# Latent attention on one core: second keys, values, head fillers and output pieces in another order

## The chip, the cores and the metric

The kernel runs on 1 core of one Trainium2 chip. The metric is device time in microseconds (us) of one execution. The kernel before took 850.55 us in the median of 3 runs (849.61 to 850.91).

## What is computed

Two transformer blocks over 256 tokens of width 1024: sliding-window attention and a gated feed-forward network, then an mLSTM and spatial-gating mixer, a feed-forward network, **latent attention**, and a last feed-forward network. Only the latent attention's order changes. Its computation, with 16 heads, 64 plain and 32 rotary features per head:

```python
def mla_mixer(h, positions, w_in, q_g, kv_g, w_uq, w_ukv, w_out):
    cq, ckv, kr = jnp.split(h @ w_in, [Q_LORA, Q_LORA + KV_LORA], axis=-1)
    q = (rms_norm_2(cq, q_g) @ w_uq).reshape(bsz, seq, C_HEADS, C_NOPE + C_ROPE)
    kv = (rms_norm_2(ckv, kv_g) @ w_ukv).reshape(bsz, seq, C_HEADS, C_NOPE + C_V)
    ...
    q_rope = apply_rope(q[..., C_NOPE:], cos, sin)
    k_rope = apply_rope(kr[:, :, None, :], cos, sin)
    qf = jnp.concatenate([q[..., :C_NOPE], q_rope], axis=-1)
    kf = jnp.concatenate([kv[..., :C_NOPE], jnp.broadcast_to(k_rope, ...)], axis=-1)
    v = kv[..., C_NOPE:]
    ...
        s = jnp.einsum("bqhd,bkhd->bhqk", qblk, kf) * scale
        pr = jax.nn.softmax(s, axis=-1)
        o = jnp.einsum("bhqk,bkhd->bqhd", pr, v)
    return o @ w_out
```

## The kernel before

All weights stream once through the core. The host packs them into units of at most 128 x 1024 numbers in the order of their use (`_weights`); SyncE loads two units at a time (`raw`, 1 MB, three buffers), and each unit is split by ScalarE into a rounded high part `wh` (line 262) and by VectorE into the rest `wl` (line 263); nine such pairs fit. A product of activations and weights is three matmuls: high by high, low by high, high by low (`mm3`, line 295; every matmul of that kind has line 293). Activations are split in the same way (`split`, lines 311 to 315: `kb` for the key latents, `xb` for the query latents, `hb` for the heads' outputs). Transposes on TensorE have line 303. PSUM has eight tiles, all called `ps`.

A scheduler sets the order of each engine's instructions from the order in the code, priorities, and what it thinks to be ready; each engine then takes its list strictly from the top and waits where an operand is missing. `self.pin` keeps the weight splits where the code has them; `self.limit` and `self.ahead` say how many units may be split ahead.

Latent attention (`mla`, line 1111) has these steps. `mla_latent` (1125) makes key latents, query latents and the shared rotary key, normalizes them and transposes the key latents (`lck`, 1160). The rotary key goes to all heads of `kT` by a DMA (1195). `mla_keys` (1213) makes the plain keys of eight heads: 24 matmuls, whose results ScalarE (1220) and VectorE (1221) copy into `kT`. `cq_finish` (1197) transposes the query latents (`lcq`). `mla_heads` (1224) then runs the heads: `rope(g4)` makes the rotary queries of four heads (ScalarE copies them to `qr`, line 1253, VectorE shuffles, 1255, GpSimd multiplies by the cosines, 1256, VectorE adds into `qT`, 1259, four adds, one for each head), `nope(g4)` their plain part (copied by ScalarE, 1240), `values(n)` half of the values (24 passes of 512 columns in all for n = 0 and 1), `soft(h)` the scores and the softmax of a head (maximum 1286, exponentials 1291, division 1295), `trans(h)` transposes the probabilities (copied at 1305), and `value(j)` multiplies two heads by the values. `out_steps` (408) gives the eight pieces of the output projection, by output half n and input quarter kp; `boundary` (377) adds them to x, transposes x and hands over to the feed-forward network.

In the code before, the keys of heads 8 to 15 come first in `mla_heads`, then rotary and plain queries of the first four heads, `values(0)`, and the loop over the heads.

Of the kernel before, what the change touches and what calls it, by code (L numbers as in the profile page):

```python
# [18 lines left out]
P = 128  # L19
# [18 lines left out]
def _pb(w, cols):  # L38
    k = w.shape[0] // P
    return w[:, cols].reshape(k, P, len(cols)).transpose(1, 0, 2).reshape(P, -1)  # L40


def _pa(w, k0, k1, c0, c1):
    return w[k0 * P : k1 * P, c0:c1].reshape(k1 - k0, P, c1 - c0).transpose(1, 0, 2).reshape(P, -1)


def _rng(a, b):
    return np.arange(a, b)


def _pair_heads(j):
    p, g = divmod(j, 4)
    return 2 * p * 4 + g, (2 * p + 1) * 4 + g


def _out_units(w):
    return [_pa(w, 2 * kp, 2 * kp + 2, 512 * n, 512 * n + 512) for n in range(2) for kp in range(4)]


def _ffn_order(nf, nin):  # L60
# [10 lines left out]
def _weights(i):  # L71
    u = []
    w = i["swa_w_in"][0]
    for p in range(2):
        u.append(_pb(w, _rng(1024 + p * P, 1024 + p * P + P)))
    for h in range(2):
        u.append(_pa(w, 4 * h, 4 * h + 4, 1280, 1536))
    for j in range(8):
        a, b = _pair_heads(j)
        u.append(_pb(w, np.concatenate([_rng(a * 64, a * 64 + 64), _rng(b * 64, b * 64 + 64)])))  # L80
    w = i["swa_w_out"][0]
    rows = np.concatenate([_rng(h * 64, h * 64 + 64) for j in range(8) for h in _pair_heads(j)])
    u += _out_units(w[rows])
    wg, wd = i["ffn_w_gate_up"][0], i["ffn_w_down"][0]
    for kind, f, s in _ffn_order(FF1 // P, 2):
        if kind == "i":
            u.append(_pb(wg, _rng(s * FF1 + f * P, s * FF1 + f * P + P)))
        else:
            u.append(wd[f * P : f * P + P])
    w = i["ab_w_in_2"][0]  # L90
    g = np.zeros((D, P), w.dtype)
    for q, r in ((1, 0), (3, 32), (0, 64), (2, 96)):
        g[:, r : r + 4] = w[:, 2048 + 4 * q : 2048 + 4 * q + 4]
    u.append(_pb(g, _rng(0, P)))
    for h in range(4):
        for s in range(2):
            c = s * 512 + h * P
            u.append(_pb(w, _rng(c, c + P)))
    for c in (1024, 1536, 2576):
        for kp in range(4):  # L100
            u.append(_pa(w, 2 * kp, 2 * kp + 2, c, c + 512))
    for m in range(4):
        u.append(_pb(w, _rng(2064 + m * P, 2064 + m * P + P)))
    u += _out_units(i["ab_w_out_2"][0])
    for layer in range(2):
        w1, w2 = i["ffn_w1_2"][layer], i["ffn_w2_2"][layer]
        if layer == 1:
            w = i["c_w_in_2"][0]
            for k0 in (0, 4):
                for c0, c1 in ((384, 672), (0, 384)):  # L110
                    u.append(_pa(w, k0, k0 + 2, c0, c1))
                    u.append(_pa(w, k0 + 2, k0 + 4, c0, c1))
            w = i["c_w_ukv_2"][0]
            for m in range(0, 8, 4):
                u.append(np.concatenate([_pb(w, np.concatenate([_rng(h * P, h * P + 64) for h in (2 * a, 2 * a + 1)])) for a in range(m, m + 4)], 1))
            vc = np.concatenate([_rng(h * P + 64, h * P + P) for h in range(NH)])
            wv = [w[kt * P : kt * P + P][:, vc] for kt in range(2)]
            w = i["c_w_uq_2"][0]
            for g4 in range(4):
                ms = [np.concatenate([_rng(h * 96, h * 96 + 64) for h in (2 * a, 2 * a + 1)]) for a in (2 * g4, 2 * g4 + 1)]  # L120
                ms.append(np.concatenate([_rng(h * 96 + 64, h * 96 + 96) for h in range(4 * g4, 4 * g4 + 4)]))
                u.append(_pb(w, ms[2]))
                u.append(np.concatenate([_pb(w, ms[0]), _pb(w, ms[1])], 1))
                if g4 == 0:
                    u += wv
            u += _out_units(i["c_w_out_2"][0])
        for kind, f, s in _ffn_order(FF2 // P, 1):
            if kind == "i":
                u.append(_pb(w1, _rng(f * P, f * P + P)))
            else:  # L130
                u.append(w2[f * P : f * P + P])
    sizes = [a.shape[1] for a in u]
    if len(u) % 2:
        u.append(np.zeros((P, UN), np.float32))
        sizes.append(0)
    out = np.zeros((len(u) // 2, P, 2, UN), np.float32)
    for n, a in enumerate(u):
        out[n // 2, :, n % 2, : a.shape[1]] = a
    return out.reshape(len(u) // 2, P, 2 * UN), sizes
# [71 lines left out]
class K:  # L211
# [1011 lines left out]

    def mla_heads(self, ckT, cqT, kT, qsc):
        nc = self.nc
        self.mla_keys(ckT, kT, 1)
        qTs, prs, pts = {}, {}, {}
        acts = []
        v = [self.t([P, D], "mlv", 2) for _ in range(2)]
# [13 lines left out]
        def rope(g4):  # L1243
            qT = qTs[g4] = self.t([96, 4, T], "qT", 2)
            w = self.unit()
            ps = self.ps()
            for k in range(3):
                s = slice(k * P, k * P + P)
                self.mm3(ps[:, :T], (w[0][:, s], w[1][:, s]), cqT[k], k == 0, k == 2)
            self.done(w)  # L1250
            with self.tc.high_priority(100) if g4 == 0 else nullcontext():
                q0 = self.t([P, T], "qr0", 2)
                nc.scalar.activation(q0, ps[:, :T], AF.Copy)
                q1 = self.t([P, T], "qr1", 2)
                nc.vector.stream_shuffle(q1, q0, self.swap)
                nc.gpsimd.tensor_tensor(out=q0, in0=q0, in1=self.cosT, op=ALU.mult)
                nc.vector.tensor_tensor(out=q1, in0=q1, in1=self.sinT, op=ALU.mult)
                for e in range(4):
                    nc.vector.tensor_tensor(out=qT[64:96, e], in0=q0[32 * e : 32 * e + 32], in1=q1[32 * e : 32 * e + 32], op=ALU.add)  # L1259
# [3 lines left out]
        def values(n):  # L1263
            if n == 0:
                wv.extend((self.unit(), self.unit()))
            for t in range(2):
                ps = self.ps()
                for k in range(2):
                    s = slice(t * P, t * P + P)
                    c = slice(n * 512, n * 512 + 512)  # L1270
                    self.mm3(ps, (ckT[k][0][:, s], ckT[k][1][:, s]), (wv[k][0][:, c], wv[k][1][:, c]), k == 0, k == 1)
                nc.scalar.activation(v[t][:, n * 512 : n * 512 + 512], ps, AF.Copy)
            if n == 1:
                for w in wv:
                    self.done(w)
# [22 lines left out]
        def trans(h):  # L1298
            pr = prs.pop(h)
            tp = self.ps()  # L1300
            for kb in range(2):
                for t in range(2):
                    self.tr(tp[:, (kb * 2 + t) * P : (kb * 2 + t + 1) * P], pr[:, t, kb * P : kb * P + P])
            pt = self.t([P, 2, T], "mpt", 3)
            nc.scalar.activation(pt.rearrange("p a b -> p (a b)"), tp, AF.Copy)
            pts[h] = pt

        def value(j):
            p = [pts.pop(2 * j), pts.pop(2 * j + 1)]
            o = self.ps()  # L1310
            for kb in range(2):
                for e in range(2):
                    h = 2 * j + e
                    self.mm(o[e * 64 : e * 64 + 64, :T], v[kb][:, h * 64 : h * 64 + 64], p[e][:, kb], kb == 0, kb == 1)
            acts.append(self.split(o[:, :T], None, "h", 8))

        steps, accs = self.out_steps(acts, {1: lambda: trans(14), 2: lambda: (trans(15), value(6)), 3: lambda: value(7)})
        self.pin = True
        first = self.used
        self.limit = first + 7  # L1320
        self.ahead = WBUFS
        rope(0)
        nope(0)
        values(0)
        for h in range(NH):
            self.limit = first + 7 + min(h, 3) + (h >= 9) + (h >= 13)
            self.load()
            soft(h)
            if h >= 3:
                trans(h - 3)  # L1330
            if h == 0:
                values(1)
            if h in (0, 4, 8):
                rope(h // 4 + 1)
            if h in (1, 5, 9):
                nope(h // 4 + 1)
            if h >= 5 and h % 2 == 1:
                value((h - 5) // 2)
            if h == 10:
                steps[0].pop(0)()  # L1340
        trans(13)
        self.limit = 1 << 30
        self.pin = False
        self.ahead = 4
        return steps, accs


    def finish(self, acc, pend, down, tiles, r2):
# [86 lines left out]
```

## Time and profile before

| what | value |
|---|---|
| median of 3 runs | 850.55 us (849.61 to 850.91) |
| the profiled execution | 851.47 us, of it 849.8 us from the first instruction to the last |
| TensorE (PE) busy | 835.0 us, 98% of the span |
| VectorE (DVE) busy | 606.6 us, 71% |
| ScalarE (ACT) busy | 510.5 us, 60% |
| GpSimd (POOL) busy | 41.5 us, 5% |
| latent attention in the trace | from about 564 us to about 662 us |

How to read it: times in the trace count from the span's first instruction. PE's busy time is modelled with a matmul's latency in it, so that a row of matmuls overlaps; a wait shorter than that latency doesn't show as idle time. In brackets behind an instruction stands how long its engine had been idle before it and what ended that. A matmul of plain 32-bit numbers (scores, values times probabilities) runs as two passes, so two matmuls are four records.

### The profile page before, as it was taken

What the parts mean: (1) busy time and instruction counts of PE and PEld (TensorE: products, weight loads), DVE (VectorE), ACT (ScalarE), POOL (GpSimd) and SP (SyncE); (2) the same over time, 40 slices, a digit from 0 to 9 for tenths busy, and PEclk for the clock granted to TensorE, in tenths of its full rate; (3) what the DMA queues carried; (4) which work ended last, traced back from release to release, by engine and by line L of the source; (5) the groups of instructions that cost most, each with busy time, mean ns of one, the idle gap of its engine ahead of it and who ended that gap; (6) DMA issues with size and microseconds to landing.
All of it is one profiled execution on the core that took longest, in us unless ns stands there. A gap on an engine that the chain in (4) does not pass through costs nothing.

```text
span 849.8 us, 12664 instructions
## 1 busy us (share of the span) xinstructions
PE 835.0 (98%) x4768; PEld 721.3 (85%) x4768; DVE 606.6 (71%) x1135; ACT 510.5 (60%) x972; POOL 41.5 (5%) x58
## 2 busy tenths in 40 slices
PE   9999999999999999999999999999999999999996
PEld 9877888888888987988888888898877888888885
DVE  5897776666766897787666766667878766666644
ACT  6696655555455969866455645456787744545532
POOL 0520000000000002200000000001000000000001
PEclk9999999999999999999999999999999999999999
DMA  9447555555554514554655555545217655555511
GB/s 328 173 163 263 179 208 191 196 180 179 196 199 148 199 51 149 199 205 148 220 184 195 195 198 197 195 169 173 85 51 245 219 206 199 198 184 175 190 47 49
DMA packets 24109, 151.41 MB, mean 178 GB/s; under 512 B 2768, under 2 KB 3536, under 8 KB 6768
## 3 DMA queue, kind: packets, MB, share of 16 engines
q1 hardware_dynamic: 23712, 149.95, 49.8%
q8 instruction: 37, 0.61, 0.3%
q10 hardware_dynamic: 288, 0.52, 0.2%
q0 software_dynamic: 48, 0.13, 0.1%
q14 instruction: 24, 0.20, 0.1%
HBM read 149.03 MB, written 1.05 MB: 177 GB/s over the span
## 4 chain that ended last, share of the span: by engine, by line
PE 78%; DVE 10%; ACT 6%; DMA 3%; issue 2%; POOL 1%; SPq 0%; POOLq 0%; DVEq 0%; ACTq 0%
PE ps L293 76%; DVE wl L263 3%; DMA raw<-in_w_dram 3%; PE ps L303 2%; ACT wh L262 1%; DMA x<-in_x_dram 1%; DVE qk L888 1%; DVE xb L315 1%; DVE sws L723 1%; ACT mpr L1291 1%; DVE sws L704 1%; ACT L890 0%; DVE qT L1259 0%; POOL r L319 0%; ACT mex L994 0%
## 5 line engine op out<-in xcount | busy, mean ns | idle before, releaser
L263 DVE TENSOR_TENSOR wl<-raw,wh 128x1024 fp32r<-128x1024 f32 (+4 forms) x278 | 329.3, 1190 | 134.8 <-ACT wh L262 128.9
L262 ACT ACTIVATE wh<-raw 128x1024 fp32r<-128x1024 f32 (+4 forms) x278 | 284.2, 1032 | 136.3 <-PE ps L293 123.0
L293 PE MATMUL ps<-xb,wh 128*128 128x512 f32 (+1 forms) x1304 | 283.5, 356 | 1.2 <-ACT wh L262 0.7
L293 PE MATMUL ps<-wh,hb 128*128 128x512 f32 (+1 forms) x944 | 280.3, 379 | 0.3 <-ACT hb L311 0.3
L293 PEld LDWEIGHTS ps<-xb,wh 128*128 128x128 f32 x1304 | 215.6, 189 | 32.9 <-DVE xb L315 1.6
L293 PEld LDWEIGHTS ps<-wh,hb 128*128 128x128 f32 x944 | 169.1, 189 | 31.9 <-issue 1.7
L293 PE MATMUL ps<-wl,hb 128*128 128x512 f32 (+1 forms) x472 | 177.6, 377 | 0.5 <-DVE wl L263 0.5
L293 PE MATMUL ps<-xb,wl 128*128 128x256 f32 x1084 | 159.3, 282 | 0.0
L293 PEld LDWEIGHTS ps<-xb,wl 128*128 128x128 f32 x1084 | 150.5, 191 | 9.4
L311 ACT ACTIVATE hb<-fp 128x256 fp32r<-128x256 f32 x90 | 36.9, 415 | 119.2 <-DVE fp L545 89.7
L293 PEld LDWEIGHTS ps<-wl,hb 128*128 128x128 f32 x472 | 88.8, 188 | 17.3 <-DVE wl L263 0.9
L312 DVE TENSOR_TENSOR hb<-fp,hb 128x256 fp32r<-128x256 f32 x90 | 37.7, 424 | 33.9 <-ACT hb L311 33.9
L447 DVE TENSOR_TENSOR fg<-ps,fg 128x256 f32<-128x256 f32 x108 | 44.6, 417 | 10.4 <-ACT fg L446 10.4
L446 ACT ACTIVATE fg<-ps 128x256 f32<-128x256 f32 x108 | 39.9, 369 | 11.1 <-PE ps L293 11.0
L293 PE MATMUL ps<-wh,xb 128*128 128x512 f32 (+3 forms) x192 | 39.8, 350 | 0.0
L293 PEld LDWEIGHTS ps<-wh,xb 128*128 128x128 f32 x192 | 31.6, 189 | 3.5
L319 POOL TENSOR_TENSOR r<-ms,mhalf 128x2 f32<-128x2 f32 x7 | 5.3, 760 | 485.4 <-DVE ms L324 485.4
L545 DVE SCALAR_TENSOR_TENSOR fp<-fg 128x256 f32<-128x256 f32 x64 | 26.8, 423 | 1.8
L314 ACT ACTIVATE xb<-ps,cols 128x256 fp32r<-128x256 f32 x35 | 15.5, 470 | 18.8 <-PE ps L303 12.9
L315 DVE SCALAR_TENSOR_TENSOR xb<-ps,cols,xb 128x256 fp32r<-128x256 f32 x35 | 16.0, 479 | 9.6 <-ACT xb L314 9.5
L293 PE MATMUL ps<-wl,xb 128*128 128x512 f32 (+3 forms) x96 | 21.4, 348 | 0.0
L1291 ACT ACTIVATE mpr<-ps,mnm,qsc 128x256 f32<-128x256 f32 x32 | 17.8, 574 | 4.3 <-DVE mnm L1287 4.2
(224 smaller groups left out, 611.0 us busy)
## 6 DMA issues: line engine op xcount, KB each, us to landing
raw<-in_w_dram SPq DMA_DIRECT2D x135, 1024.0 KB, 4.7
raw<-in_w_dram SPq DMA_DIRECT2D x4, 512.0 KB, 7.2
xraw<-in_xt_dram SPq DMA_DIRECT2D x4, 257.0 KB, 4.9
raw<-in_w_dram SPq DMA_DIRECT2D x4, 256.0 KB, 5.6
x<-in_x_dram SPq DMA_DIRECT2D x4, 256.0 KB, 6.5
row_fn<-in_fn_dram SPq DMA_DIRECT2D x2, 512.0 KB, 6.2
kT<-kr SPq DMA_DIRECT2D x1, 512.0 KB, 4.6
out_dram<-fo SPq DMA_DIRECT2D x2, 256.0 KB, 2.0
```

Of the source, the lines that this page charges most:

```text
L262: a = self.nc.scalar.activation(hi[:, c], raw[:, c], AF.Copy)
L263: b = self.nc.vector.tensor_tensor(out=lo[:, c], in0=raw[:, c], in1=hi[:, c].bitcast(F32), op=ALU.subtract)
L293: self.nc.tensor.matmul(out, lhsT, rhs, start=start, stop=stop)
L303: self.nc.tensor.transpose(out, in_, self.ident)
L311: self.last_act = nc.scalar.activation(hi, src, AF.Copy)
L312: self.last_dve = nc.vector.tensor_tensor(out=lo, in0=src, in1=hi.bitcast(F32), op=ALU.subtract)
L314: self.last_act = nc.scalar.activation(hi, src, AF.Copy, scale=scale)
L315: self.last_dve = nc.vector.scalar_tensor_tensor(out=lo, in0=src, scalar=scale, in1=hi.bitcast(F32), op0=ALU.mult, op1=ALU.subtract)
L446: self.nc.scalar.activation(out, ps[:, T:], AF.Copy)
L447: self.nc.vector.tensor_tensor(out=out, in0=ps[:, :T], in1=out, op=ALU.add)
L545: nc.vector.scalar_tensor_tensor(out=p, in0=g, scalar=0.0, in1=g, op0=ALU.max, op1=ALU.mult)
L1291: nc.scalar.activation(pr[:, t], s3[:, t], AF.Exp, scale=qsc[:, t : t + 1], bias=nm[:, t : t + 1], accum_out=den[:, t : t + 1])
```

## The change

Nothing is computed that was not computed before. What moves:

- the weights of the second keys (heads 8 to 15) come behind those of the first queries, and `mla_keys(ckT, kT, 1)` behind `rope(0)` and `nope(0)`;
- `values(0)` moves from ahead of the first scores to behind them, `values(1)` and the next queries one head later; a table `between` lists what stands behind each head's scores, and `value` comes ahead of it;
- the number of units that may be split ahead grows by a table `split`, head by head;
- a second output piece moves between the heads (behind head 13), and the last heads' transposes and products are put between output pieces of both halves (`late`), whose weights are packed in the order `LATE`.

```diff
+PLAIN = tuple((n, kp) for n in range(2) for kp in range(4))
+LATE = ((0, 0), (0, 1), (0, 2), (1, 0), (1, 1), (0, 3), (1, 2), (1, 3))
+
+def _out_units(w, order=PLAIN):
+    return [_pa(w, 2 * kp, 2 * kp + 2, 512 * n, 512 * n + 512) for n, kp in order]
...
             w = i["c_w_uq_2"][0]
+            u.append(keys[0])
             for g4 in range(4):
...
                 if g4 == 0:
+                    u.append(keys[1])
                     u += wv
-            u += _out_units(i["c_w_out_2"][0])
+            u += _out_units(i["c_w_out_2"][0], LATE)
...
     def mla_heads(self, ckT, cqT, kT, qsc):
         nc = self.nc
-        self.mla_keys(ckT, kT, 1)
...
-        steps, accs = self.out_steps(acts, {1: lambda: trans(14), 2: lambda: (trans(15), value(6)), 3: lambda: value(7)})
+        steps, accs = self.out_steps(acts, {})
...
+        between = {
+            0: (lambda: values(0),),
+            1: (lambda: rope(1), lambda: values(1)),
+            2: (lambda: nope(1),),
+            4: (lambda: rope(2),),
+            5: (lambda: nope(2),),
+            8: (lambda: rope(3),),
+            9: (lambda: nope(3),),
+            10: (steps[0][0],),
+            13: (steps[0][1],),
+        }
+        split = {1: 1, 2: 1, 5: 1, 6: 1, 7: 1, 9: 1, 11: 1, 13: 1, 14: 1, 15: 1}
         rope(0)
         nope(0)
-        values(0)
+        self.mla_keys(ckT, kT, 1)
         for h in range(NH):
-            self.limit = first + 7 + min(h, 3) + (h >= 9) + (h >= 13)
+            self.limit += split.get(h, 0)
             self.load()
             soft(h)
             if h >= 3:
                 trans(h - 3)
-            if h == 0:
-                values(1)
-            if h in (0, 4, 8):
-                rope(h // 4 + 1)
-            if h in (1, 5, 9):
-                nope(h // 4 + 1)
             if h >= 5 and h % 2 == 1:
                 value((h - 5) // 2)
-            if h == 10:
-                steps[0].pop(0)()
+            for f in between.get(h, ()):
+                f()
         trans(13)
...
-        return steps, accs
+
+        def late():
+            steps[0][2]()
+            trans(14)
+            steps[1][0]()
+            trans(15)
+            value(6)
+            steps[1][1]()
+            value(7)
+            steps[0][3]()
+
+        return ([late], steps[1][2:]), accs
```

What the built program makes of it, at three places. Line numbers of the changed kernel are higher by 7 or 8; numbers behind a name are buffers.

**Latents, VectorE and TensorE.** VectorE before, from the norm of the inputs to the key latents `lck`:

```order
L1141 TENSOR_TENSOR r_733_5947<-r_5941 128x2
L263 TENSOR_TENSOR wl_6106<-raw_5923,wh_6105 128x1024
L1148 TENSOR_TENSOR lkvs_5949<-lkvs_5949,r_733_5947 128x2
L324 TENSOR_SCALAR lkvm_5956<-lkvs_5949 128x2
L1152 TENSOR_TENSOR lkvq_5959<-lkvr_5955,r_5941 128x2
L1160 TENSOR_SCALAR lck_5961<-ps_5819,lkvq_5959 128x256
```

VectorE now:

```order
L1149 TENSOR_TENSOR r_733_5947<-r_5941 128x2
L1156 TENSOR_TENSOR lkvs_5949<-lkvs_5949,r_733_5947 128x2
L332 TENSOR_SCALAR lkvm_5956<-lkvs_5949 128x2
L1160 TENSOR_TENSOR lkvq_5959<-lkvr_5955,r_5941 128x2
L1168 TENSOR_SCALAR lck_5961<-ps_5819,lkvq_5959 128x256
```

TensorE now, at the transposes of the query latents (`xb_6085` is the first third of them, split); before, nine matmuls of the second keys stood where the six with `xb_6085` stand:

```order
L311 MATMUL ps_6082<-cols,lcq_6029 128x128
L311 MATMUL ps_6082<-cols,lcq_6031 128x128
L311 MATMUL ps_6093<-cols,lcq_6029 128x128
L311 MATMUL ps_6093<-cols,lcq_6031 128x128
L301 MATMUL ps_6122<-xb_6085,wh_5925 128x256
L301 MATMUL ps_6122<-xb_6085,wl_5926 128x256
L301 MATMUL ps_6142<-xb_6085,wh_5969 128x256
L301 MATMUL ps_6142<-xb_6085,wl_5970 128x256
L301 MATMUL ps_6154<-xb_6085,wh_5969 128x256
L301 MATMUL ps_6154<-xb_6085,wl_5970 128x256
L311 MATMUL ps_6082<-cols,lcq_6029 128x128
L311 MATMUL ps_6082<-cols,lcq_6031 128x128
```

One weight split left the chain of the key latents; the second keys left the gap between the query transposes.

**First scores, TensorE and ScalarE.** TensorE before, from the last plain queries (`ps_6194`) over `values(0)` to the first scores (`kT,qT`):

```order
L293 MATMUL ps_6194<-xb_6096,wh_5987 128x256
L293 MATMUL ps_6206<-wh_6042,kb_6004 128x512 x2
L293 MATMUL ps_6206<-wl_6043,kb_6004 128x512
L293 MATMUL ps_6206<-wh_6105,kb_6007 128x512 x2
L293 MATMUL ps_6206<-wl_6106,kb_6007 128x512
L293 MATMUL ps_6214<-wh_6042,kb_6004 128x512 x2
L293 MATMUL ps_6214<-wl_6043,kb_6004 128x512
L293 MATMUL ps_6214<-wh_6105,kb_6007 128x512 x2
L293 MATMUL ps_6214<-wl_6106,kb_6007 128x512
L293 MATMUL ps_6222<-kT_5812,qT_6147 128x256 x2
```

TensorE now, from the last of the second keys (`ps_6193`):

```order
L301 MATMUL ps_6193<-kb_6007,wl_5988 128x256
L301 MATMUL ps_6193<-kb_6007,wh_5987 128x256
L301 MATMUL ps_6202<-kT_5812,qT_6105 128x256 x2
L301 MATMUL ps_6217<-wh_6042,kb_6004 128x512 x2
L301 MATMUL ps_6217<-wl_6043,kb_6004 128x512
L301 MATMUL ps_6217<-wh_6108,kb_6007 128x512 x2
```

ScalarE before, from the copies of the second keys to the rotary queries `qr`:

```order
L1220 ACTIVATE kT_5812<-ps_6136 64x256
L262 ACTIVATE wh_6148<-raw_5923 128x384
L262 ACTIVATE wh_6154<-raw_5985 128x768
L262 ACTIVATE wh_6158<-raw_5985 128x384
L1253 ACTIVATE qr_775_6172<-ps_6162 128x256
L1240 ACTIVATE qT_6147<-ps_6182 64x256 x2
```

ScalarE now:

```order
L270 ACTIVATE wh_6118<-raw_5985 128x768
L1228 ACTIVATE kT_5812<-ps_6166 64x256
L1228 ACTIVATE kT_5812<-ps_6175 64x256
L1228 ACTIVATE kT_5812<-ps_6184 64x256
L1228 ACTIVATE kT_5812<-ps_6193 64x256
L1260 ACTIVATE qr_771_6132<-ps_6122 128x256
L1247 ACTIVATE qT_6105<-ps_6142 64x256 x2
```

On TensorE the twelve matmuls of `values(0)` went from ahead of the first scores to behind them. On ScalarE the rotary queries' copy stands behind the copy of the last keys, whose matmuls are the last ones ahead of the scores.

**Last heads, VectorE.** Before, from the product of heads 10 and 11 (`hb_6789`) to that of heads 12 and 13 (`hb_6850`) and of 14 and 15 (`hb_6874`):

```order
L312 TENSOR_TENSOR hb_6789<-ps_6784,hb_6789 128x256
L263 TENSOR_TENSOR wl_6806<-raw_6338,wh_6805 128x1024
L263 TENSOR_TENSOR wl_6810<-raw_6338,wh_6809 128x1024
L263 TENSOR_TENSOR wl_6835<-raw_6704,wh_6834 128x1024
L312 TENSOR_TENSOR hb_6850<-ps_6845,hb_6850 128x256
L263 TENSOR_TENSOR wl_6866<-raw_6704,wh_6865 128x1024
L263 TENSOR_TENSOR wl_6894<-raw_6803,wh_6893 128x1024
L312 TENSOR_TENSOR hb_6874<-ps_6869,hb_6874 128x256
```

Now, from the product of heads 10 and 11 (`hb_6821`):

```order
L320 TENSOR_TENSOR hb_6821<-ps_6816,hb_6821 128x256
L1302 TENSOR_SCALAR mpr_6801<-mpr_6801,mrc_6805 128x256 x2
L271 TENSOR_TENSOR wl_6851<-raw_6562,wh_6850 128x1024
L271 TENSOR_TENSOR wl_6886<-raw_6714,wh_6885 128x1024
L271 TENSOR_TENSOR wl_6910<-raw_6714,wh_6909 128x1024
L271 TENSOR_TENSOR wl_6930<-raw_6788,wh_6929 128x1024
L271 TENSOR_TENSOR wl_6973<-raw_6788,wh_6972 128x1024
L320 TENSOR_TENSOR hb_6880<-ps_6875,hb_6880 128x256
L271 TENSOR_TENSOR wl_6998<-raw_6883,wh_6997 128x1024
L271 TENSOR_TENSOR wl_7002<-raw_6883,wh_7001 128x1024
L320 TENSOR_TENSOR hb_6906<-ps_6901,hb_6906 128x256
```

Five weight splits instead of three stand ahead of heads 12 and 13.

## Rows read from the trace of the kernel before

**Rows 1.** The page: the span, and busy time, share and count of each engine.

```profile
span 849.8 us, 12664 instructions
PE 835.0 (98%) x4768; PEld 721.3 (85%) x4768; DVE 606.6 (71%) x1135; ACT 510.5 (60%) x972; POOL 41.5 (5%) x58
```

**Rows 2.** Busy time in a stretch of the heads: PE, PEld, DVE, ACT, POOL (us), clock, DMA.

```profile
606.00:624.00 18.00, 18.00 (x129) 15.05 (x128) 16.38 (x51) 16.78 (x50) 1.78 (x2) 1.00 0.17 60
```

**Rows 3.** Timeline, PE, latents to second scores: start, length, instruction, count, [idle before].

```profile
579.65 0.55 PE L303 MATMUL ps<-cols,lck 128*128 128x128 f32 x3 [0.21 <-DVE lck L1160]
...
584.07 0.60 PE L303 MATMUL ps<-cols,lcq 128*128 128x128 f32 x4
...
586.21 0.44 PE L303 MATMUL ps<-cols,lcq 128*128 128x128 f32 x2 [0.51 <-DVE xb L315]
...
591.31 0.28 PE L293 MATMUL ps<-xb,wh 128*128 128x256 f32 x1
591.43 0.62 PE L293 MATMUL ps<-wh,kb 128*128 128x512 f32 x2
...
594.18 1.03 PE L293 MATMUL ps<-kT,qT 96*128 96x256 f32 x4
```

**Rows 4.** Timeline, PE: later waits into the last network, and one product of two heads.

```profile
605.67 0.33 PE L303 MATMUL ps<-cols,mpr 128*128 128x128 f32 x1 [0.56 <-DVE mpr L1295]
...
625.31 0.50 PE L293 MATMUL ps<-wl,hb 128*128 128x512 f32 x1 [0.50 <-DVE wl L263]
...
642.11 1.08 PE L293 MATMUL ps<-mpt,mlv 128*64 128x256 f32 x8
...
649.08 1.21 PE L293 MATMUL ps<-wh,hb 128*128 128x512 f32 x4 [0.31 <-ACT hb L311]
...
670.42 0.50 PE L293 MATMUL ps<-xb,wh 128*128 128x512 f32 x1 [0.52 <-DVE xb L315]
```

**Rows 5.** Timeline, ACT: first query latents, last key copy, first rotary queries.

```profile
584.55 0.46 ACT L314 ACTIVATE xb<-ps,cols 128x256 fp32r<-128x256 f32 x1
...
588.41 0.38 ACT L1220 ACTIVATE kT<-ps 64x256 f32<-64x256 f32 x1 [0.30 <-PE ps L293]
...
590.25 0.36 ACT L1253 ACTIVATE qr<-ps 128x256 f32<-128x256 f32 x1
```

**Rows 6.** Timeline, DVE: the latents, the first query latents, the rotary queries.

```profile
575.90 1.22 DVE L263 TENSOR_TENSOR wl<-raw,wh 128x1024 fp32r<-128x1024 f32 x1
577.04 0.15 DVE L1148 TENSOR_TENSOR lkvs<-lkvs,r 128x2 f32<-128x2 f32 x1
...
585.67 0.48 DVE L315 SCALAR_TENSOR_TENSOR xb<-ps,cols,xb 128x256 fp32r<-128x256 f32 x1
...
591.33 0.44 DVE L1255 STREAM_SHUFFLE qr<-qr 128x256 f32<-128x256 f32 x1
...
592.86 1.76 DVE L1259 TENSOR_TENSOR qT<-qr,qr 32x256 f32<-32x256 f32 x4 [0.64 <-POOL qr L1256]
```

**Rows 7.** Timeline, POOL: cosines of the first and last rotary queries.

```profile
591.84 0.99 POOL L1256 TENSOR_TENSOR qr<-qr,cosT 128x256 f32<-128x256 f32 x1 [8.27 <-DVE qr L1255]
...
620.88 0.82 POOL L1256 TENSOR_TENSOR qr<-qr,cosT 128x256 f32<-128x256 f32 x1 [8.77 <-DVE mnm L1287]
```

**Rows 8.** Waits of PE over the whole span, the longest: in total, times, longest.

```profile
PE ps L293 <- DVE mh L1021: 1.4, 1, 1.4
```

**Rows 9.** Timeline, PE: the first matmuls, transposes in the heads, the last matmul.

```profile
1.10 5.49 PE L293 MATMUL ps<-ones 128*128 128x128 f32 x26 [1.10 <-POOL ones L600]
...
608.21 0.60 PE L303 MATMUL ps<-cols,mpr 128*128 128x128 f32 x4
...
842.76 0.28 PE L293 MATMUL ps<-wl,hb 128*128 128x256 f32 x1
```

**Rows 10.** Busy time in the last two stretches, columns as in rows 2.

```profile
843.00:845.60 2.60, 0.04 (x1) 0.00 (x0) 2.04 (x6) 1.82 (x6) 1.74 (x2) 1.00 0.27 101
845.60:849.80 4.20, 0.00 (x0) 0.00 (x0) 0.27 (x1) 0.50 (x1) 0.00 (x0) 0.51 0.50 187
```

More of the change, by code (lines that the diff above doesn't have):

```diff
@@ L53, in _pair_heads @@
     return 2 * p * 4 + g, (2 * p + 1) * 4 + g
-def _out_units(w):
-    return [_pa(w, 2 * kp, 2 * kp + 2, 512 * n, 512 * n + 512) for n in range(2) for kp in range(4)]
+PLAIN = tuple((n, kp) for n in range(2) for kp in range(4))
+LATE = ((0, 0), (0, 1), (0, 2), (1, 0), (1, 1), (0, 3), (1, 2), (1, 3))
+def _out_units(w, order=PLAIN):
+    return [_pa(w, 2 * kp, 2 * kp + 2, 512 * n, 512 * n + 512) for n, kp in order]
 def _ffn_order(nf, nin):
@@ L113, in _weights @@
             w = i["c_w_ukv_2"][0]
+            keys = []
             for m in range(0, 8, 4):
-                u.append(np.concatenate([_pb(w, np.concatenate([_rng(h * P, h * P + 64) for h in (2 * a, 2 * a + 1)])) for a in range(m, m + 4)], 1))
+                keys.append(np.concatenate([_pb(w, np.concatenate([_rng(h * P, h * P + 64) for h in (2 * a, 2 * a + 1)])) for a in range(m, m + 4)], 1))
             vc = np.concatenate([_rng(h * P + 64, h * P + P) for h in range(NH)])
```

## The prediction

> **What bounds the kernel now.** I read the page's busy times first: PE is busy 835.0 of 849.8 us, the other engines at most 71% [rows 1]. The windows by stretch say how near the others are: in the heads DVE is busy 16.38 and ACT 16.78 of 18 us while PE never waits [rows 2], so they keep up with little to spare. The kernel lasts as long as PE's work and PE's waits, and an edit that leaves PE's work alone can only add or remove waits. Then PE's list in both orders, from the latents to the first feed-forward matmuls: the same 497 instructions, with 70 changes between plain and rounded operands before and 68 now. PE's work is equal; the sum is one of waits.
>
> So I went through PE's timeline for waits. From the latents to the first network six are left: ahead of the key latents' transposes, between the query latents' transposes [rows 3], at the second head's transposes, at the first output piece, at the last output input, and in the network behind [rows 4]. The idle time in brackets is too short. The matmul at 591.31 lasts 0.28 us, yet the next starts 0.12 later [rows 3], so 0.16 of each wait hides in the last matmul's latency. With it the first is 0.37, the second 0.67, the later four 0.72, 0.66, 0.47 and 0.68 us: 2.53 together. All six are 3.57 us, and no reordering of this stage can win more.
>
> Last, I read ACT, DVE and POOL around the places that move [rows 5 to 7].
>
> **The change, part by part.** The profiled execution took 851.47 us, 0.92 more than the median; I make the sum against it and carry the difference over to the median.
>
> *Key latents.* The split of the second values' weights no longer stands on DVE between the input norm and the squares' product. In the trace that split starts at 575.90, lasts 1.22 us, and the product follows at its end [rows 6]; the transposes were waiting for what comes of it. Without it the chain has about 0.5 us in hand, more than the wait of 0.37: **-0.37**. The split itself goes behind the query latents, where ACT and DVE are between copies; it is done 1 us before the last keys reach those engines, so I cost it at nothing. If that cover were gone it would cost its 1.2 us on DVE.
>
> *Query latents.* Before, nine matmuls of the second keys filled the gap between the first four and the last two transposes, and PE still waited 0.67 us, until DVE's low half of the first third (from 585.67, 0.48 long) was written [rows 3, 6]. Now six matmuls stand there that need the first third itself. The four transposes are issued by 584.51 (start 584.07, 0.11 each); ACT's high half ends at 585.01 [rows 5], so PE waits 0.55, works six times 0.12, and waits 0.46 for the low half. 1.0 instead of 0.67: **+0.33**. Bounds: 0 if the high half is early, 0.6 if the later thirds wait as well.
>
> *First scores.* Before, the rotary queries' chain over ACT, DVE, POOL and DVE ran beside the twelve matmuls of values(0), 591.43 to 594.18, 2.75 us [rows 3]. Now PE comes to the first scores right behind the second keys, at about 591.4 again (-0.37 + 0.33 leaves it where it was, since the same 51 matmuls are done). But ACT has the copy of the last keys ahead of the rotary queries. So the chain starts only when PE's last key matmul ends: 0.28 for that matmul [rows 3], 0.38 for the copy of the keys, 0.36 for that of the queries [rows 5], 0.51 from the shuffle's start to POOL's, 0.99 on POOL [rows 6, 7], 0.44 for the first of four adds (1.76 / 4). That is 2.96; about 0.15 for handing over four times, less 0.12 in which PE would have been busy: **+3.0**. In the trace the scores started at 594.18, before the adds ended at 594.62 [rows 3, 6], so one add is enough. Bounds: 2.6 (the shorter POOL row, 0.82 [rows 7], and copies that overlap) and 4.3 (all four adds needed). I take 3.0, since each piece has its row. values(0) then stands behind the scores and covers the first softmax. No other work covers this wait: behind the first scores PE's whole list is queued.
>
> *Later waits.* PE now has a value or query block between the first scores, so the probabilities that the second head's transposes wait for come some 4 us ahead of them: -0.72. The first output piece's weights are split at head 7, not 9, with more than 4 us in hand: -0.66. The last product's halves come behind six matmuls of the last first-half piece and five of the next: -0.47. In the network behind, the second half's transposes now come before the first matmuls have run out, and their halves are needed some 2 us after they are there: -0.68. Together **-2.53**. Bounds: 0, if each wait comes back in another place, and -2.53. I take the whole, since at each place I count at least 0.4 us in hand.
>
> *Transfers.* As many weight loads as before; each waits for the pair three before it to be split, and with earlier splits two of them get ahead of the final norm's row on SP. PE waits for no load now, and the loads come earlier: nothing.
>
> Sum: -0.37 + 0.33 + 3.0 - 2.53 = +0.43. For this execution 851.9, for the median 850.55 + 0.43 = **851.0 us**: the gains pay for the new wait.
>
> **The rivals.**
>
> *The clock falls in the new wait (slower).* PE waits nowhere longer than 1.4 us [rows 8], and its clock stays at the upper level, 2.4 GHz. At the end its last matmul ends at 843.04 [rows 9]; in the stretch up to 845.6 the granted clock is still 1.00, in the one behind it 0.51, the lower level, 1.2 GHz [rows 10]. So PE loses the clock when it stops, after idling about as long as the new wait lasts. At the start, out of rest, 26 passes took 5.49 us, 0.21 each, where transposes of the same size later go at 0.11 [rows 9]. If the work behind the wait ran that way for as long, it would lose half of it, 2.7 us at most, and nothing if the level holds. Part of the slow spell would lie in the wait itself, so I take 1.8: **852.8 us**. It decides if the new wait is no shorter than that last idling was when the clock fell. Against it: PE works right up to the wait and at once after it, while at the end it never came back.
>
> The Trainium skill has the rule (TensorE: Matmul & The Clock Gate, Part 1: The HAM clock gate): a monitor "sets K/N based on how busy the PE has been recently", with half rate as the state of rest. Both ends of this trace agree; no run here yet shows it in the middle of the kernel. By the rule the time is that of this rival, by the granted clock of the heads as it is now that of the forecast.
>
> *The late splits hold up the last heads (slower, or at the edge).* Five instead of three splits of 1.2 us [rows 6] stand on DVE ahead of the low half of heads 12 and 13: from the last probabilities on 6.0 + 0.4 us. PE has about 5.2 us of work in that time: a set of transposes, 0.44 [rows 9], two products of 1.0 [rows 4], twelve matmuls of together 2.75 [rows 3]. It comes to them some twelve matmuls after DVE begins, so about 1.5 us are in hand; it decides if DVE, nearly full in the heads [rows 2], falls further behind than that. Price 0 to 1.9, I take 1.3, nearer the upper end, since a late DVE stays late there: **852.3 us**.
>
> *The change does what its words say: the first scores' wait is covered (faster).* Then 3.0 falls away: 850.55 + 0.43 - 3.0 = **848.0 us**. For it, only that something else on PE could be ready; against it, the order: nothing else stands there on PE's list, and ACT takes the last keys first.
>
> **How the numbers follow.** Forecast 0.55, clock 0.26, late splits 0.12, covered 0.07. A measurement of this kernel can tell 0.2%, 1.7 us, from no change: below 848.85 is faster, above 852.25 slower. Faster: the covered case, nearly whole: 0.06. Slower: most of the clock case (0.22), half of the late splits (0.06), and 0.06 of the forecast with some later waits kept: 0.34. Same: 0.60. The range goes down to 849.6 (the wait at its lower bound, and 0.9 below for where the three runs lay) and up to 853.3, which takes in the late splits and the clock case up to 2.3 of its 2.7 us; it leaves out the covered case and the worst of the clock.
>
> **What would show it.** Right: PE waits near 591 to 594 us for DVE, some 3 us in one piece; no wait ahead of the key latents; two short ones at the query latents; none of the four later ones; the granted clock 1.00 throughout. The clock case: under 1.00 in the slice around 595, and matmuls of 512 columns twice as far apart there. Late splits: PE idle near 653 for DVE's low half of heads 12 and 13. Wrong altogether: no wait of over 2 us at the first scores, or new waits for ACT between 605 and 625.

## The result, and the profile after

The changed kernel takes 854.48 us (median of 4 runs, 853.94 to 854.70), the kernel before beside it 850.12 us (849.61 to 850.91): ratio 1.0052, 95% interval 1.0040 to 1.0063. It is slower by 4.4 us, outside the range, where the forecast was slower by 0.4. One execution of all that follow, in e1, took 1680 us, twice as long as the rest, and counts in no comparison.

The page of the changed kernel, the counts of [rows 1]:

```profile
PE 836.5 (98%) x4768; PEld 722.3 (85%) x4768; DVE 607.5 (71%) x1135; ACT 511.4 (60%) x972; POOL 41.2 (5%) x58
```

The counts of work are the same, so waits and clock are all there is. Among what PE waited for in the whole span (in total, times, longest):

```profile
PE ps L301 <- ACT qT L1247: 2.8, 1, 2.8
...
PE ps L301 <- ACT mpt L1312: 0.2, 1, 0.2
```

The new wait of 2.8 us is the one that was forecast. The four later waits of [rows 4] are gone; one for `mpt` is new. PE's timeline of the changed kernel (start, length, instruction, count, [idle before]): first norm's transposes, key latents, query latents, last key matmul, first and second scores, the products (`mpt,mlv`) and the last matmul:

```profile
558.93 0.38 PE L311 MATMUL ps<-cols,x 128*128 128x128 f32 x2
...
578.57 0.60 PE L311 MATMUL ps<-cols,lck 128*128 128x128 f32 x4
...
583.04 0.60 PE L311 MATMUL ps<-cols,lcq 128*128 128x128 f32 x4
584.03 0.39 PE L301 MATMUL ps<-xb,wh 128*128 128x256 f32 x1 [0.39 <-ACT xb L322]
...
584.71 0.28 PE L301 MATMUL ps<-xb,wl 128*128 128x256 f32 x1
585.18 0.44 PE L311 MATMUL ps<-cols,lcq 128*128 128x128 f32 x2 [0.19 <-DVE xb L323]
...
590.83 0.28 PE L301 MATMUL ps<-kb,wh 128*128 128x256 f32 x1
593.92 1.20 PE L301 MATMUL ps<-kT,qT 96*128 96x256 f32 x4 [2.82 <-ACT qT L1247]
...
599.22 1.03 PE L301 MATMUL ps<-kT,qT 96*128 96x256 f32 x4
...
617.97 1.35 PE L301 MATMUL ps<-mpt,mlv 128*64 128x256 f32 x8
623.13 1.28 PE L301 MATMUL ps<-mpt,mlv 128*64 128x256 f32 x8
...
635.86 0.65 PE L301 MATMUL ps<-mpt,mlv 128*64 128x256 f32 x2
636.70 1.08 PE L301 MATMUL ps<-mpt,mlv 128*64 128x256 f32 x6 [0.20 <-ACT mpt L1312]
...
845.09 0.28 PE L301 MATMUL ps<-wl,hb 128*128 128x256 f32 x1
```

The chain in front of the scores, on ACT and DVE (its first and its last links):

```profile
591.14 0.38 ACT L1228 ACTIVATE kT<-ps 64x256 f32<-64x256 f32 x1 [0.30 <-PE ps L301]
591.42 0.36 ACT L1260 ACTIVATE qr<-ps 128x256 f32<-128x256 f32 x1
...
593.41 1.76 DVE L1266 TENSOR_TENSOR qT<-qr,qr 32x256 f32<-32x256 f32 x4 [0.61 <-POOL qr L1263]
```

The scores start at 593.92, behind the first of the four adds (593.41 + 1.76 / 4 = 593.85); ACT, which the profile names, was done with its first copies before. That is 3.09 us after the matmul ahead of them. From the first scores to the second, with `values(0)` between them, it takes 5.30 us. Three products run longer than the 1.08 us of [rows 4]. The windows of that place (PE, PEld, DVE, ACT, POOL, granted clock, DMA) show the clock:

```profile
590.00:594.00 4.00, 1.18 (x11) 1.01 (x9) 3.01 (x10) 2.60 (x8) 0.91 (x1) 1.00 0.70 262
594.00:598.00 4.00, 4.00 (x12) 3.17 (x13) 2.51 (x8) 1.48 (x5) 0.00 (x0) 0.60 0.00 0
598.00:602.00 4.00, 4.00 (x23) 3.54 (x22) 1.68 (x6) 1.97 (x5) 0.00 (x0) 0.97 0.00 0
...
594.00:596.00 2.00, 2.00 (x7) 1.65 (x8) 1.87 (x5) 0.00 (x0) 0.00 (x0) 0.70 0.00 0
```

PE idled most of the first stretch, yet the granted clock there is 1.00. In the second stretch it is 0.60, so most of it ran at 1.2 GHz; then it is back at 2.4 GHz. The last line is the first half of that second stretch: 0.70, which leaves 0.50 for the other half. So the clock did not fall in the wait, but behind 594, when PE was at work again. This can't be seen on the page, whose 40 slices of 21 us show a 9 there.

### The profile page after: what moved, and what is told of

Same layout as the page of the kernel before. It is cut to its first block, busy times and chain, and to the rows that moved or that the text cites. A ratio compares the mean times of both kernels' runs of the same rounds, so it can differ in the third digit from the quotient of the medians.

```text
span 852.2 us, 12654 instructions
## 1 busy us (share of the span) xinstructions
PE 836.5 (98%) x4768; PEld 722.3 (85%) x4768; DVE 607.5 (71%) x1135; ACT 511.4 (60%) x972; POOL 41.2 (5%) x58
## 4 chain that ended last, share of the span: by engine, by line
PE 85%; DVE 7%; ACT 5%; issue 2%; DMA 1%; POOL 0%; ACTq 0%; SPq 0%; DVEq 0%
PE ps L301 83%; DVE wl L271 2%; PE ps L311 2%; DVE qk L896 1%; DVE sws L731 1%; ACT wh L270 1%; DMA xraw<-in_xt_dram 1%; DVE sws L712 1%; ACT L898 0%; ACT mpr L1298 0%; DVE xb L323 0%; ACT mex L1002 0%; ACT L1002 0%; ACT qk L898 0%; DVE x L851 0%
```

## The experiments

Theory A: the new wait costs its length and, on top, time at the lower clock. Theory B: the wait alone. Theory C: the extra time comes from the later half of the change (splits, fillers, pieces). Times are medians; each group of runs has its own runs of the kernel before.

**e1 and e6: the same wait, with PE kept busy.** Behind `mla_keys(ckT, kT, 1)`:

```diff
+        ps = self.ps()
+        for _ in range(22):
+            self.mm(ps[:, :T], ckT[0][0][:, :P], ckT[0][0])
```

> The changed kernel with 22 spare matmuls of 256 columns (some 2.4 us, read by nobody) behind the last of the second keys, ahead of the first scores: PE is busy in most of the 2.8 us wait, and the scores come no earlier. Theory A (the wait itself and, on top, some 1.7 us of work at the lower clock behind it): the granted clock stays at 1.00 around 595 us, matmuls of 512 columns there at 0.21 us, time 1.7 us under the changed kernel's, about +2.7 us against the kernel before. Theory B (the wait alone, the fall of the clock costs nothing): as the changed kernel, +4.4 us.

852.40 us (9 runs) against 850.00 before: 1.0027, 1.0017 to 1.0037. The trace is that of e6, one more execution of the same kernel, which took 853.03 us, 0.6 over e1's median:

> As e1_warm, for its profile, since the profiled execution of that one was disturbed and shows no clock. Theory A: granted clock 1.00 in every slice from 580 to 610 us, matmuls of 512 columns behind the first scores 0.21 us apart, and the first scores start as late as in the changed kernel. Theory B: the clock falls as there, or it does not fall and the time is still +4.4.

PE's timeline of e6, and its window behind the wait:

```profile
591.48 2.80 PE L301 MATMUL ps<-kb 128*128 128x256 f32 x22
594.61 1.10 PE L301 MATMUL ps<-kT,qT 96*128 96x256 f32 x4 [0.33 <-PE ps L301]
...
598.31 1.03 PE L301 MATMUL ps<-kT,qT 96*128 96x256 f32 x4
```

```profile
594.00:598.00 4.00, 3.67 (x18) 2.97 (x17) 2.51 (x7) 1.24 (x5) 0.00 (x0) 1.00 0.02 4
```

The first scores start 3.13 us behind the first spare matmul, so no earlier than in the changed kernel. But the clock is 1.00, and from the first scores to the second it takes 3.70 us (594.61 to 598.31) instead of 5.30 (593.92 to 599.22). The same work, with work of no use in place of idling, is 1.60 us faster. From the norm's transposes to the last matmul e6 takes 284.72 us (559.44 to 844.16), 1.44 less than the changed kernel's 286.16 below, since its wait is 0.16 longer. By the ratios to before the difference is 0.25%, 2.1 us. Theory A holds, B falls.

**e2: the wait filled with useful work.**

```diff
         self.mla_keys(ckT, kT, 1)
+        values(0)
         for h in range(NH):
...
-            0: (lambda: values(0),),
```

> The changed kernel with values(0) back ahead of the first scores, all else as changed. Theory A (wait and clock): the wait shrinks from 2.8 to about 0.4 us and the clock stays at 1.00: 2.6 + 1.7 us less than the changed kernel, about 0.0 us against before. Theory B (wait alone): 2.6 us less, +1.8. Theory C (the extra time is in the heads and the output, from the new order of splits and pieces): less than 2 us gained, over +2.4, with new waits on PE behind 605 us.

850.48 us (11 runs) against 850.00: 1.0004, 0.9995 to 1.0013. One moved call takes back nearly the whole loss, by theory A's number. In its trace PE waits 0.23 us ahead of the first scores, and the clock is 1.00 from 590 to 602.

**e3: the later half alone.** The kernel before with the tables `between` and `split`, `late` and `LATE`; the second keys and `values(0)` where they were, and one unit less allowed to be split ahead at the start than in the changed kernel (`first + 6`). The products stand ahead of the fillers, as in the changed kernel.

> The kernel before with the later half of the change alone: the table of splits, the values and queries one head later, the second output piece between the heads, the late order of pieces; the second keys and values(0) stay where they were. Theory A: the four later waits go (2.5 us), nothing takes their place: -2.5 us against before. Theory C (the later half costs time): 0 or slower, with waits on PE behind 605 us.

849.77 us (11 runs) against 850.00: 0.9998, 0.9989 to 1.0006. On the whole the later half costs nothing, but gains nothing either. Theory A's -2.5 us fails. What came is the mild end of theory C's case, "0 or slower, with waits on PE behind 605 us": this half doesn't carry the loss, but part of it is lost here. PE's timeline of e3 at the first product, and below it ACT's:

```profile
607.84 0.65 PE L300 MATMUL ps<-mpt,mlv 128*64 128x256 f32 x2
609.13 1.08 PE L300 MATMUL ps<-mpt,mlv 128*64 128x256 f32 x6 [0.65 <-ACT mpt L1312]
...
632.49 1.70 PE L300 MATMUL ps<-mpt,mlv 128*64 128x256 f32 x8
```

```profile
607.93 0.56 ACT L1298 ACTIVATE mpr<-ps,mnm,qsc 128x256 f32<-128x256 f32 x1
...
608.48 0.60 ACT L1312 ACTIVATE mpt<-ps 128x512 f32<-128x512 f32 x1
```

The product stands right behind a set of transposes and needs `mpt`, which ACT copies only behind the exponentials. It ends at 610.21 (609.13 + 1.08), 2.37 us after its start: 1.3 more than 1.08. The one at 632.49 takes 0.6 more. About 1.9 us of the gain is given back here.

**e7: the products back behind the fillers.** e3 with

```diff
-            if h >= 5 and h % 2 == 1:
-                value((h - 5) // 2)
             for f in between.get(h, ()):
                 f()
+            if h >= 5 and h % 2 == 1:
+                value((h - 5) // 2)
```

> e3_late_part with the products of two heads back behind the fillers (the next queries), as before the change. If e3's gain was lost because a product now stands right behind a set of transposes, with nothing for PE to do while ACT, behind three heads' exponentials, copies what the product reads: the two waits at products (0.6 and 1.3 us in e3) go, and the time is 1.5 to 1.9 us under e3, -1.7 to -2.2 against before. If the loss in e3 is elsewhere: as e3, -0.2.

848.82 us (11 runs) against 849.95: 0.9988, 0.9980 to 0.9997. The time is 0.95 us under e3's, not 1.5 to 1.9. PE's timeline of e7 shows why:

```profile
609.40 1.08 PE L300 MATMUL ps<-mpt,mlv 128*64 128x256 f32 x8
613.22 1.80 PE L300 MATMUL ps<-mpt,mlv 128*64 128x256 f32 x8
```

The first product runs without a wait, as do those behind 620; the second product, which has no filler ahead of it, waits 0.7, where e3 had no wait (1.08 at 615.08). So 1.9 less 0.7, 1.2 us, is won back by the trace. The mechanism holds, its size was too large. This kernel is the fastest of those tried, 0.12% under the kernel before.

**e5: the kernel before, profiled again.** Its profiled execution had taken 0.92 us more than the median of the three runs on record, and 1.47 more than that of 25 later ones (850.00).

> The kernel before, profiled once more, since its profiled execution took 851.47 us and the median of its 25 timed runs is 850.0. Theory F (that execution had longer waits than most): the stage from the latents to the first network, 103.5 us there from the start of the matmul at 570.05 to that of the one at 673.57, is about 1 us shorter, and one or more of the four later waits (2.5 us together) are smaller. Theory G (the waits belong to the order of the work): the same waits within 0.1 us, the same 103.5 us, and the difference lies ahead of 570 us.

850.14 us. PE's timeline (first norm's transposes, key latents, query latents, second head, first output piece, last matmul; no other wait shows in between), and ACT's split of weights ahead of the last output input, once in the first profile of the kernel before and once in this one:

```profile
559.59 0.38 PE L303 MATMUL ps<-cols,x 128*128 128x128 f32 x2
...
579.21 0.30 PE L303 MATMUL ps<-cols,lck 128*128 128x128 f32 x1
579.71 0.55 PE L303 MATMUL ps<-cols,lck 128*128 128x128 f32 x3 [0.20 <-DVE lck L1160]
...
585.55 0.28 PE L293 MATMUL ps<-kb,wh 128*128 128x256 f32 x1
586.26 0.44 PE L303 MATMUL ps<-cols,lcq 128*128 128x128 f32 x2 [0.43 <-DVE xb L315]
...
605.78 0.33 PE L303 MATMUL ps<-cols,mpr 128*128 128x128 f32 x1 [0.56 <-DVE mpr L1295]
...
625.42 0.50 PE L293 MATMUL ps<-wl,hb 128*128 128x512 f32 x1 [0.50 <-DVE wl L263]
...
841.44 0.28 PE L293 MATMUL ps<-wl,hb 128*128 128x256 f32 x1
```

```profile
647.70 1.06 ACT L262 ACTIVATE wh<-raw 128x1024 fp32r<-128x1024 f32 x1 [1.53 <-DMA raw<-in_w_dram]
```

```profile
647.30 1.06 ACT L262 ACTIVATE wh<-raw 128x1024 fp32r<-128x1024 f32 x1 [1.01 <-DMA raw<-in_w_dram]
```

Theory F holds. From the norm's transposes to the last matmul the first profile took 283.25 us (559.51 to 842.76 [rows 9]), this one 281.85. The waits at the last output input and in the network, 0.47 and 0.68, are not there. They came behind a split that waited 1.53 us for its weights instead of 1.01: half a microsecond in the landing of one load. That this load made both is read from their order; no run tests it. Two of my four later waits belonged to that execution.

**e4: a shorter chain.** The rotary queries of heads 0 to 3 in memory of their own:

```diff
+        self.q0s = [self.t([P, T], f"qz{i}", 1) for i in range(2)]
...
-                q0 = self.t([P, T], "qr0", 2)
+                q0 = self.q0s[0] if g4 == 0 else self.t([P, T], "qr0", 2)
```

and the same for `q1`.

> The changed kernel with the rotary queries of the first four heads in memory of their own, not in that of the rotary key that a transfer still reads: their copy on ACT then stands ahead of the second keys' copies. If the chain over ACT, DVE, POOL and DVE set the wait because its copy came last: the chain runs beside the second keys, the wait falls from 2.8 to about 1.1 us (the last key copy and one query copy, 0.4 each, and the handing over). Theory A (wait and clock): -1.8 and -1.7, about +0.9 us against before; theory B (wait alone): +2.6. If the chain is not what is waited for: no change, +4.4.

854.23 us (5 runs) against 850.00: 1.0045, 1.0032 to 1.0057; not told apart from the changed kernel. The copy did move ahead, but PE's wait only fell to 2.2 us. DVE's timeline of e4, and its windows from the wait on:

```profile
589.64 0.95 DVE L271 TENSOR_TENSOR wl<-raw,wh 128x768 fp32r<-128x768 f32 x1
590.62 1.45 DVE L1230 COPY kT<-ps 64x256 f32<-64x256 f32 x4
592.10 1.76 DVE L1267 TENSOR_TENSOR qT<-qz,qz 32x256 f32<-32x256 f32 x4
```

```profile
592.00:596.00 4.00, 3.38 (x8) 2.76 (x9) 2.59 (x7) 0.63 (x2) 0.00 (x0) 0.55 0.24 96
596.00:600.00 4.00, 4.00 (x12) 3.12 (x12) 0.78 (x3) 1.85 (x6) 0.00 (x0) 0.60 0.00 0
```

The chain's last step now queues on DVE behind a weight split and four key copies. And the clock is low in both stretches where the changed kernel had it low in one: the wait shrank by 0.6 us, but from the first scores (592.62) to the second (599.43) it takes 6.81 us instead of 5.30. By its time this would be the expected case "the chain is not what is waited for"; the trace shows that it still is, and that a longer spell took back what the shorter wait gave.

**e9 and e10: shorter waits.** e9 is the changed kernel with half of `values(0)` on each side of the first scores; e10 is the kernel before with `values(0)` behind them and no other edit.

```diff
         self.mla_keys(ckT, kT, 1)
+        values(0, (0,))
...
-            0: (lambda: values(0),),
+            0: (lambda: values(0, (1,)),),
```

> The changed kernel with the first half of values(0), six matmuls of 512 columns (1.4 us), ahead of the first scores and the second half behind them: the wait is 1.6 us instead of 3.0, as the chain ends when it did. If a wait of this length keeps the clock: 1.4 + 1.6 us under the changed kernel, +1.3 against before. If the clock falls in it too: only 1.4 less, or nothing where the fall lasts longer, +3.0 or more.

> The kernel before with one move alone: values(0) behind the first scores. The rotary queries' copy on ACT stands where it stood (590.25 us, ahead of nothing late), so the scores can start at about 593.4 and PE, done with the plain queries at 591.5, waits 1.9 us; the second head's transposes get 2.7 us of work more ahead of them and lose their wait of 0.8. If the clock stays: +1.1 us against before; if it falls: 1.7 to 3.4 us more, +2.8 to +4.5.

e9: 851.52 us (10 runs) against 849.96: 1.0021, 1.0012 to 1.0029. e10: 852.68 (5 runs): 1.0035, 1.0023 to 1.0048. PE's timeline and the window of e9:

```profile
594.09 1.10 PE L301 MATMUL ps<-kT,qT 96*128 96x256 f32 x4 [1.56 <-ACT mlv L1279]
```

```profile
592.00:596.00 4.00, 2.44 (x12) 1.76 (x11) 3.19 (x9) 1.83 (x5) 0.91 (x1) 1.00 0.33 139
```

The same of e10:

```profile
594.86 1.10 PE L293 MATMUL ps<-kT,qT 96*128 96x256 f32 x4 [1.76 <-ACT qT L1240]
```

```profile
592.00:596.00 4.00, 2.24 (x15) 1.96 (x14) 3.28 (x9) 1.58 (x5) 0.96 (x1) 1.00 0.92 295
```

With 1.56 and 1.76 us of idling the clock stays at 2.4 GHz, and e9's time, +1.6 us, is near the +1.3 of the case without a fall. e10 warns against reading the time alone: +2.7 is nearest to what I had given for a fall (+2.8 to +4.5), but in its trace the clock did not fall. The wait is there; the gain of 0.8 at the second head did not come, which makes 1.9 of the 2.7. The rest stays open: the profiled execution took 854.91 us, 2.2 more than the median, and in it ACT waits 1.96 us for a weight load ahead of the last output input, as in the first profile of before.

**e11: the first half alone.** e10 with `mla_keys(ckT, kT, 1)` and its weights behind the first queries, and one unit more allowed to be split ahead from head 1 on.

> e10 with the second keys moved behind the first queries as well: the first half of the change without the second (splits, fillers, pieces and products as in the kernel before). Theory A (the first half carries the loss): wait 3.0, clock 1.6, query latents +0.35, key latents -0.45, the second head's wait -0.8, no new wait at the products: +3.7 us against before. Theory C (most of it is in the later half): under +2.

855.03 us (6 runs) against 849.96: 1.0062, 1.0047 to 1.0077. The first half carries the whole loss. It is 1.4 us more than expected: the second head's transposes, which I thought would lose their wait, wait 1.1 us for `mpr` now. The window behind the first scores and PE's timeline at the second head:

```profile
594.00:598.00 4.00, 4.00 (x12) 3.15 (x12) 1.98 (x6) 1.26 (x5) 0.00 (x0) 0.57 0.00 0
```

```profile
610.25 0.33 PE L306 MATMUL ps<-cols,mpr 128*128 128x128 f32 x1 [1.11 <-DVE mpr L1297]
```

The wait at the first scores is 2.82 us again, and the clock falls again. The second head's wait is cured by the later half's fillers, not by `values(0)`: the changed kernel, which has both, does not have it.

**e8: the two smaller edits on top of e7.** The rotary queries' memory as in e4, and in `mla`, ahead of the latents,

```diff
+        self.limit = 196
```

> e7 with the split of the second values' weights taken out of the key latents' chain (it comes behind the query latents, as in the changed kernel, but the second keys stay ahead of the queries), and the rotary queries of the first heads in memory of their own, so that their copy on ACT stands ahead of the splits. If the key latents' wait of 0.37 us came from that split alone: 0.4 us less than e7 and no wait there. If the split now holds up the first queries or values(0): a new wait between 588 and 594 us and nothing gained.

849.53 us (11 runs) against 849.95: 0.9995, 0.9986 to 1.0004. No gain over e7 that could be told. In its trace the key latents' wait is gone, as expected, but short waits for `mpt` (0.25) and `mpr` (0.16) stand in the heads that e7 does not have; whether they belong to the kernel was not tried.

**e12: the changed kernel, profiled again.**

> The changed kernel, profiled once more. If what its first profile shows belongs to the kernel: the stage from the latents to the network within 0.3 us of 106.45, the wait of 2.8 us for the first queries, the granted clock at the lower level in or behind that wait (its length and start may differ), and a wait of about 0.5 us at the product near 636. If the fall of the clock is an accident of that execution: 1.00 there and a stage of about 104.8.

853.91 us. PE's timeline at both scores, and the window behind the first:

```profile
593.95 1.62 PE L301 MATMUL ps<-kT,qT 96*128 96x256 f32 x4 [2.82 <-ACT qT L1247]
...
599.26 1.03 PE L301 MATMUL ps<-kT,qT 96*128 96x256 f32 x4
```

```profile
594.00:598.00 4.00, 4.00 (x11) 3.17 (x12) 2.15 (x6) 1.20 (x4) 0.00 (x0) 0.57 0.00 0
```

The same wait, and 5.31 us between the scores: the fall is no accident of one execution.

## Why the prediction was wrong

The changed kernel against the second profile of the kernel before, term by term; each from starts of matmuls in the fences above, less what the matmul itself takes. For the second head and the first piece the starts ahead of the waits are 604.19 and 624.20; the matmuls there take 0.87 and 0.54.

| term | forecast | measured | from |
|---|---|---|---|
| key latents | -0.37 | -0.39 | 579.21 to 579.71, less 0.11; no wait now |
| query latents | +0.33 | +0.31 | 0.55 + 0.35 now, 0.59 before |
| first scores | +3.0 | +2.97 | 590.83 to 593.92, less 0.12 |
| clock behind them | 0 | +1.60 | 5.30 in the changed kernel, 3.70 in e6 |
| second head, first piece | -1.38 | -1.40 | 0.72 and 0.68, both gone |
| last input, network | -1.15 | 0 | not there in the second profile |
| products | 0 | +1.31 | 0.27 + 0.20 + 0.84 over 1.08 |
| sum | +0.43 | +4.40 | |

The stretch from the norm's transposes to the last matmul is 286.16 us in the changed kernel and 281.85 in the second profile of before: +4.31, of which the terms explain all but 0.1. The medians differ by 4.36.

*Right:* the three terms at the front, each within 0.03 us. The new wait was worked out link by link, and stood where it was said. That it came so near is in part luck: POOL took 0.91 us instead of 0.99 and ACT's two copies overlapped by 0.1, while handing over from engine to engine took about 0.1 more than I had put. At the query latents the second wait was 0.35, not 0.46, but the wait before was 0.59, not 0.67. I named one cause of the wait, ACT's order, with the keys' copies ahead of the rotary queries'. e4 shows that it is not the only one: without it DVE's key copies hold the chain, and 2.2 of the 2.8 us stay.

*Wrong, the clock (1.6 us).* I set the rival "the clock falls in the new wait" at 0.26 and priced it at 1.8; it was the case that came, at 1.6. The step that failed is "Against it: PE works right up to the wait and at once after it, while at the end it never came back". Coming back at once protects nothing: the granted clock was 1.00 through the whole wait and fell to the lower level when PE was at work again, so the work that came back ran in it. The price was near by luck. It let part of the slow spell lie in the wait, and none of it did, and the spell behind 594 was over by 598 (0.97), shorter than the start's 5.49 us. The rule of the Trainium skill (TensorE: Matmul & The Clock Gate, Part 1: The HAM clock gate), which I had named beside the rival, is borne out here by the 0.60 and 0.57 in the windows behind the wait, and by 1.00 where e6 kept PE busy. The deciding point that I gave ("if the new wait is no shorter than that last idling was") was met by my own numbers, 3.0 us against 845.6 - 843.04 = 2.6 [rows 9, 10]. I should have given it the larger chance.

*Wrong, the later waits (1.15 us).* The step was to take all four waits of one profiled execution as the kernel's. I had noted that it took 0.92 us more than the median, and carried that difference over as a constant beside the sum. It was no constant: two of the waits that I counted as gain are 1.15 of the 1.40 us by which the two profiles differ. A slow profile lends a change gains that it can't make.

*Wrong, the products (1.3 us).* "At each place I count at least 0.4 us in hand" looked at the places where waits had been. The diff also put `value` ahead of the fillers, and for that I checked no place. The bound of the term ("0, if each wait comes back in another place") held the answer: e3 gains nothing in time, and e7, which undoes that one move, gains 0.95 us.

*The other rivals.* Late splits: neither trace of the changed kernel has a wait for `hb` at the last heads, so that case fell. That the wait is covered fell with the first line of the waits.

## What to carry to other kernels

A filler that covers a chain on other engines covers the clock too: before moving it, add to the wait the price of the work behind it at half rate, and if PE must idle for some 2 us or more (here 1.76 us kept the clock and 2.18 us did not, in one execution each), test whether spare matmuls there bring the clock back. Profile the kernel before twice when the sum is made of waits of half a microsecond, and count only the waits that both executions have. When the order around a consumer changes, check what now stands between it and its producer, also where no wait was before.

## What the runs showed of the hardware that was not expected

The wait's length does not say what the clock costs. After 1.56 us (e9) and 1.76 us (e10) of idling PE kept 2.4 GHz in these profiles; after 2.82 us (the changed kernel twice, and e11) it ran one stretch of 4 us at 0.60, 0.57 and 0.57; after only 2.18 us (e4) two stretches in a row were at 0.55 and 0.60. What sets the length of the spell was not tried. One of the four timed executions of the changed kernel has a mean clock of 0.999, the others 0.995, and was no faster (854.68 us); it left no trace. The mean does not tell such a short fall: e12's execution has 0.997 with the fall, and runs of the kernel before have 0.997 to 0.999. So whether the clock falls in every execution stays open. The longest wait of the kernel before, 1.4 us [rows 8], lies on the harmless side of all of these.

Spare matmuls, whose results nobody reads, made the kernel faster by 0.25% (e1 against the changed kernel, by their ratios to before), though they shorten no wait.
